# Output projection and down projection with channels on the partitions, in a hybrid encoder layer

## The chip, the cores and the metric

One Trainium2 chip, one core. The metric is the device time of one execution in microseconds. Several executions give a median; one more is recorded by the hardware profiler, and its trace gives the busy times, the waits and the timeline quoted below.

## The reference

One encoder layer over 2048 tokens of 1024 channels in float32: three token mixers on one normalised input, gated and summed to y; then an output projection into the residual stream and an MLP with squared relu. Only the end matters here:

```python
y = (gates[:, :, 0] * (h_m @ w_proj_mlstm)
     + gates[:, :, 1] * (h_na @ w_proj_na)
     + gates[:, :, 2] * (h_mem @ w_proj_mem))
x = x + y @ w_out                                # (2048, 1024)
u = rmsnorm(x, g_ffn) @ w_up                     # (2048, 4096)
return x + jnp.square(jax.nn.relu(u)) @ w_down
```

rmsnorm divides by the root of the mean square over channels, plus 1e-6, and multiplies by the gain g_ffn.

## The kernel before

**Precision.** Every large product is three matmuls (`mm3`, L230): an operand is split into a rounded high part and the rest (ScalarE copies the high part, VectorE subtracts), and high x high, high x low and low x high are summed in PSUM. These are lines L235 to L237. A split of 512 columns is thus one ScalarE and one VectorE instruction.

**Phases.** Phase 1 computes the input projections, the neighbourhood and memory attention; phase 2 the mLSTM; phase 3 the rest, for two pairs of blocks of 512 tokens (blocks 3 and 2, then 1 and 0). A pair goes through four stages:

- `merge` multiplies the three branch outputs with their projections, weights stationary, applies the gates, and leaves yT: channels on partitions, 512 tokens along, high and low. The first block's yT lies in the buffer `hT`, the second's in the buffers that are later b21 (high) and t4 (low).
- `out_proj` (L1342) multiplies by w_out. Now a tile of 128 tokens of yT is stationary and 512 output channels of w_out are moving, so the result has tokens on partitions: 2 halves of the channels x 2 blocks x 4 token tiles = 16 groups of 24 matmuls. Each group adds x (L1364), multiplies by g_ffn along the channels (L1366), stores the new x to scratch `x2`, and sums squares by ScalarE with an accumulator (L1370).
- `operands` (L1379), queued as a job, transposes each result by four matmuls with the identity (L1386), since the MLP wants channels on partitions, and makes from it the operands of a Strassen product in Winograd's form: the token half (block) and channel half give b11, b21, b12, b22 and sums t1 to t4, each split into high and low (`split`, L1390; `less`, L1394; `more`, L1401).
- `mlp_up` (L1423), 16 times per pair: seven products of 12 matmuls, sums on VectorE, squared relu (L1457), results and their sums to scratch. `mlp_down` (L1470): seven products again for each of 4 quarters of the hidden width, 48 matmuls each, summed in `acc` (L1535); here hidden activations are stationary and w_down moving, so tokens are on partitions. In the last quarter, four of the products are the last for their part of the output: x2 is loaded (L1540), one multiply-add scales by the reciprocal mean square of the token, a scalar per partition, and adds x2 (L1542), and the result is stored. The root is absent because relu is squared.

**What sets the order.** TensorE runs in the order of the program. `tick`, called after every second step of a product, runs one entry of a list of jobs; `operands` of a group is entered so that it comes at least `LATER_3 = 4` ticks after it, about one group. The other engines' queues, and SyncE's, which issues all DMAs, are ordered ahead of time by a list scheduler: by readiness and by a priority that follows the program, with a few shifts (eviction `SOON` = 40 earlier, weight splits `LATER` = 60 later, mlp_down's splits `LATER_A` = 60 later). Buffers with waiting users: five for split weights (`WSP`), eight of 128x512 for evictions (`ev`), eight PSUM banks. mlp_down prefetches its operands six steps ahead, in the first pair four and then two steps ahead towards the end, when buffers are given to the next merge (`rings`).

`u` is a buffer in the place of hT that holds mlp_up's sums (`utmp`, `usum`) and two result tiles (`uout`). `gbc` is 128x1024 and holds g_ffn on all partitions in this phase.

Of the kernel before, what the change touches and what calls it, by code (L numbers as in the profile page):

```python
# [13 lines left out]
F32 = mybir.dt.float32  # L14
F32R = mybir.dt.float32r
BF16 = mybir.dt.bfloat16
AF = mybir.ActivationFunctionType
# [5 lines left out]
D = 1024  # L23
# [28 lines left out]
def units(g):  # L52


    def navm(w):
        return [(np.concatenate([w[q:q + 256, 2064:2576], w[q:q + 256, 1536:1552]], axis=1)
                 .reshape(2, 128, 528).transpose(1, 0, 2), 2) for q in range(0, 1024, 256)]

    def ch(w):
        return [(w[:, c:c + 128].reshape(8, 128, 128).transpose(1, 0, 2), 8) for c in range(0, w.shape[1], 128)]  # L60

    def tok(w):
        return [(w[q:q + 256, c:c + 512].reshape(2, 128, 512).transpose(1, 0, 2), 2)
                for c in range(0, w.shape[1], 512) for q in range(0, w.shape[0], 256)]
    win = g["w_in"]
    return dict(w_mem_kv=tok(g["w_mem_kv"]), naqk=tok(win[:, 1552:2064]), qk=ch(win[:, 0:512]),
                v=tok(win[:, 512:1024]),
                gate=ch(win[:, 2576:5648]), o=tok(win[:, 1024:1536]),
                proj=ch(np.concatenate([g["w_proj_mlstm"], g["w_proj_na"], g["w_proj_mem"]])),
                w_out=tok(g["w_out"]), up=ch(g["w_up"]), down=tok(g["w_down"]), navm=navm(win))  # L70

# [12 lines left out]
class Body:  # L84
# [206 lines left out]
    def scratch(self):  # L291
# [19 lines left out]
            hT={b: d(f"s_hT{b}", [128, 2, 8, TB]) for b in SPILL},  # L311
            x2=[d(f"s_x2{b}", [TB, D]) for b in range(NB)],

# [953 lines left out]
    def phase_3(self):  # L1267
# [10 lines left out]
        mix = [[planes("b11"), planes("t2")], [planes("t3"), planes("b22")]]  # L1278
        self.ss = self.p_a.tile([128, 2, 16], F32, name="ss3")
        self.r2 = self.p_a.tile([128, 16], F32, name="r23")  # L1280
# [8 lines left out]
        for i in range(0, NB, 2):  # L1289
# [5 lines left out]
            self.merge(pair, mix, yT)  # L1295
            self.out_proj(pair, yT)

            u = self.p_h.tile([128, 8192], F32, name=f"u{i}", tag="hT", bufs=1)
            self.utmp = [u[:, k * 512:k * 512 + 512] for k in range(4)]
            self.usum = u[:, 2048:4096].rearrange("p (s t) -> p s t", s=4)  # L1300
            self.uout = [u[:, 4096 + k * 2048:6144 + k * 2048].rearrange("p (u i t) -> p u i t", u=2, i=2) for k in range(2)]
            for q in range(FF // 256):
# [38 lines left out]

    def out_proj(self, pair, yT):  # L1342

        nc, a = self.nc, self.a
        for half in range(2):
            w = self.take(4)
            hs = slice(half * 512, half * 512 + 512)
            for j, b in enumerate(pair):  # L1350
                for t in range(4):
                    x = self.ev()
                    r0 = b * TB + t * 128
                    nc.sync.dma_start(x, a["x"][r0:r0 + 128, hs])
                    p = self.ps("mm")
                    ts = slice(t * 128, (t + 1) * 128)
                    for k in range(8):
                        wk = w[k // 2]
                        self.mm3(p, (yT[j][0][:, k, ts], yT[j][1][:, k, ts]), (wk[:, 0, k % 2], wk[:, 1, k % 2]), k == 0, k == 7)
                        if k % 2:  # L1360
# [3 lines left out]
                    nc.vector.tensor_tensor(x, x, p, ALU.add)  # L1364
                    xh = self.ev()
                    nc.vector.tensor_tensor(xh, x, self.gbc[:, hs], ALU.mult)  # L1366
                    self.tc.cur_priority += SOON
                    self.store(self.scr["x2"][b][t * 128:(t + 1) * 128, hs], x)
                    n = 4 * b + t
                    nc.scalar.activation(self.t("ev", [128, 512], EV[3], BF16), x, AF.Square, accum_out=self.ss[:, half, n:n + 1])  # L1370
                    self.jobs += [None] * (LATER_3 - len(self.jobs) - 1)
                    self.jobs.append(lambda xh=xh, half=half, j=j, t=t: self.operands(xh, half, j, t))
        for b in pair:
            r = self.r2[:, 4 * b:4 * b + 4]
            nc.vector.tensor_tensor(r, self.ss[:, 0, 4 * b:4 * b + 4], self.ss[:, 1, 4 * b:4 * b + 4], ALU.add)
            nc.vector.tensor_scalar(r, r, 1.0 / D, EPS, ALU.mult, ALU.add)
            nc.vector.reciprocal(r, r)

    def operands(self, xh, half, j, t):  # L1379


        nc, X = self.nc, self.X
        ts = slice(t * 128, (t + 1) * 128)
        p = self.ps("mm").rearrange("p (a b) -> p a b", b=128)
        for i in range(4):
            nc.tensor.transpose(p[:, i], xh[:, i * 128:(i + 1) * 128], self.ident)  # L1386
        part = lambda x, l: X[x][:, l, :, ts]
        f32 = lambda x, l: part(x, l).bitcast(F32)

        def split(x, src):  # L1390
            nc.scalar.activation(part(x, 0), src, AF.Copy)
            nc.vector.tensor_tensor(part(x, 1), src, f32(x, 0), ALU.subtract)

        def less(src, x):  # L1394

            e = self.ev().rearrange("p (a b) -> p a b", b=128)
            nc.vector.tensor_tensor(e, src, f32(x, 0), ALU.subtract)
            nc.vector.tensor_tensor(e, e, f32(x, 1), ALU.subtract)
            return e

        def more(x, src):  # L1401

            e = self.ev().rearrange("p (a b) -> p a b", b=128)
            nc.vector.tensor_tensor(e, f32(x, 0), src, ALU.subtract)
            nc.vector.tensor_tensor(e, e, f32(x, 1), ALU.add)
            return e
        if half == 0 and j == 0:

            split("t1", p)
        elif half == 0:  # L1410
            split("b11", p)
            split("t1", more("t1", p))
        elif j == 0:
            t2 = less(p, "t1")
            split("b22", p)
            split("t2", t2)
            split("t3", less(t2, "b11"))
        else:
            t4 = less(p, "t2")
            split("b21", p)  # L1420
            split("t4", t4)

# [47 lines left out]
    def mlp_down(self, i, pair, then):  # L1470
# [43 lines left out]
        for q in range(0, FF // 256, 4):  # L1514
            for _, _, s, more, out in products:
                for dq in range(4):
                    if dq % 2 == 0:
# [11 lines left out]
                last = q == FF // 256 - 4 and (out, s, more) in ((0, 1, False), (3, 0, True), (1, 1, True), (2, 0, True))  # L1529
                for t, p in enumerate(sets[s]):  # L1530
                    c = acc[:, out, t]
                    if out not in seen:
                        nc.scalar.activation(c, p, AF.Copy)
                    else:
                        nc.vector.tensor_tensor(c, c, p, ALU.add)  # L1535
                    if last:
                        j, half = out // 2, out % 2
                        hs, r0 = slice(half * 512, half * 512 + 512), t * 128
                        x = self.ev()
                        nc.sync.dma_start(x, self.scr["x2"][pair[j]][r0:r0 + 128, hs])  # L1540
                        n = 4 * pair[j] + t
                        nc.vector.scalar_tensor_tensor(x, c, self.r2[:, n:n + 1], x, ALU.mult, ALU.add)  # L1542
                        r0 += pair[j] * TB
                        self.store(self.a["out"][r0:r0 + 128, hs], x)
                seen.add(out)
# [42 lines left out]
def layout(inp):  # L1588
# [9 lines left out]
        x=g["x"], mem=g["mem"], g_mix=bc(g["g_mix"]), gT_mix=g["g_mix"].reshape(8, 128).T,  # L1598
        xT=g["x"].reshape(16, 128, 8, 128).transpose(0, 3, 2, 1).reshape(16, 128, D), g_ffn=bc(g["g_ffn"]), g_mem=g["g_mem"].reshape(8, 128).T, memT=g["mem"].T,
        w_units=wu, w_navm=wn, b_if=bif,  # L1600
# [22 lines left out]
```

## Time and profile before

| | |
|---|---|
| median of 3 runs | 2894.17 us (2893.63 to 2894.92) |
| profiled execution, its own time | 2894.83 us |
| its span, first to last instruction | 2893.1 us |
| mean granted TensorE clock | 0.998 |
| VectorE (DVE) busy | 2004.3 us |
| ScalarE (ACT) busy | 1187.3 us |
| phase 3, first projection group to last instruction | from 1388.78 us on |

How to read the lines: a group of instructions stands as line, engine, operation, output <- inputs, shapes and count, then busy time in us and mean ns of one, then the idle time ahead of it and what ended it. A timeline row is start, duration, engine, line, operation, tiles, count, and in brackets the idle time before it with its releaser. Tiles carry the program's names without numbers, and some are named by the buffer that they share: ws are split weights, wr raw ones, mm a PSUM bank, X and B the buffers of the Strassen operands. L235 to L237 stand in a helper and are told apart by their tiles.

### The profile page before, as it was taken

Reading aid. Unit: us, or ns where it says so; the run is one execution under the profiler, and the core shown is the slowest. Engines: PE = TensorE matmul, PEld = TensorE weight load, DVE = VectorE, ACT = ScalarE, POOL = GpSimd, SP = SyncE. Lnnn points to the kernel's source line nnn. Section 1 sums busy time; section 2 is a strip of 40 time slices with the busy share of each in tenths; the row PEclk is TensorE's granted clock in tenths of the full one; section 3 lists DMA queues with packets and bytes.
Section 4 is the critical chain, followed back from the end, with each engine's and each line's share of the span. In section 5 each row is a group of like instructions: output and inputs, shape, how many; then the busy total and the mean of one; then the engine's idle time right before and its main releaser. Section 6 shows DMA issues by size and latency. Waiting matters only on the chain.

```text
span 2893.1 us, 41875 instructions
## 1 busy us (share of the span) xinstructions
PE 2861.0 (99%) x15052; PEld 2364.8 (82%) x15052; DVE 2004.3 (69%) x3438; ACT 1187.3 (41%) x2256; POOL 216.4 (7%) x382
## 2 busy tenths in 40 slices
PE   8999999999999999999999999999999999999999
PEld 6878788878877888888888888888888888888887
DVE  6676765567765555647598888666785988885666
ACT  7465654344543443532243334443322433344331
POOL 4121310011000122310000000000000000000000
PEclk9999999999999999999999999999999999999999
DMA  8786778877899888978344446656863444476654
GB/s 281 227 270 203 226 231 259 259 222 231 270 306 299 269 258 283 308 261 272 117 137 158 160 146 238 224 189 228 301 205 113 144 148 160 151 249 202 196 188 160
DMA packets 345153, 632.79 MB, mean 219 GB/s; under 512 B 29456, under 2 KB 151248, under 8 KB 344944
## 3 DMA queue, kind: packets, MB, share of 16 engines
q1 hardware_dynamic: 344944, 630.10, 67.5%
q8 instruction: 119, 1.95, 0.3%
q14 instruction: 90, 0.74, 0.1%
HBM read 453.37 MB, written 176.62 MB: 218 GB/s over the span
## 4 chain that ended last, share of the span: by engine, by line
PE 89%; DVE 3%; issue 3%; DMA 3%; ACT 1%; POOL 0%; SPq 0%; DVEq 0%; POOLq 0%; ACTq 0%
PE mm L235 27%; PE mm L237 27%; PE mm L236 27%; PE tr L1105 1%; PE pn L882 1%; PE mx L1086 1%; PE mx L1119 1%; PE pn L885 1%; PE mx L891 1%; DVE ws L180 1%; DMA nav<-s_vna 1%; PE mx L1258 1%; PE tr L1248 1%; DMA xt<-in_xT_dram 0%; DMA wr<-in_w_units_dram 0%
## 5 line engine op out<-in xcount | busy, mean ns | idle before, releaser
L235 PE MATMUL mm<-X,ws 128*128 128x512 f32 x896 | 349.0, 389 | 0.0
L237 PE MATMUL mm<-X,ws 128*128 128x512 f32 x896 | 348.6, 389 | 0.0
L236 PE MATMUL mm<-X,ws 128*128 128x512 f32 x896 | 348.6, 389 | 0.0
L180 DVE TENSOR_TENSOR ws<-wr,ws 128x1024 fp32r<-128x1024 f32 (+1 forms) x194 | 240.0, 1244 | 127.4 <-ACT ws L179 126.2
L235 PE MATMUL mm<-hT,ws 128*128 128x512 f32 (+1 forms) x712 | 283.0, 397 | 0.7 <-ACT ev L565 0.7
L237 PE MATMUL mm<-hT,ws 128*128 128x512 f32 (+1 forms) x712 | 277.0, 389 | 0.0
L236 PE MATMUL mm<-hT,ws 128*128 128x512 f32 (+1 forms) x712 | 276.7, 389 | 0.0
L235 PE MATMUL mm<-ws,hT 128*128 128x512 f32 (+2 forms) x704 | 258.3, 367 | 3.5 <-ACT zif L529 2.7
L237 PE MATMUL mm<-ws,hT 128*128 128x512 f32 (+2 forms) x704 | 249.6, 355 | 2.2 <-DVE hT L438 2.2
L179 ACT ACTIVATE ws<-wr 128x1024 fp32r<-128x1024 f32 (+1 forms) x194 | 204.1, 1058 | 111.1 <-PE mm L237 76.0
L236 PE MATMUL mm<-ws,hT 128*128 128x512 f32 (+2 forms) x704 | 248.7, 353 | 0.0
L237 PE MATMUL mm<-X 128*128 128x512 f32 x616 | 239.7, 389 | 0.2 <-DVE X L1509 0.2
L236 PE MATMUL mm<-X 128*128 128x512 f32 x616 | 239.6, 389 | 0.0
L235 PE MATMUL mm<-X 128*128 128x512 f32 x616 | 239.6, 389 | 0.0
L205 ACT ACTIVATE ws<-wr 128x512 fp32r<-128x512 f32 x224 | 135.0, 628 | 220.1 <-PE mm L237 139.5
L1508 ACT ACTIVATE X<-X 128x1024 fp32r<-128x1024 f32 x109 | 115.6, 1062 | 202.6 <-DMA X<-s_a 67.2
L237 PEld LDWEIGHTS mm<-X,ws 128*128 128x128 f32 x896 | 168.2, 188 | 35.0
L235 PEld LDWEIGHTS mm<-X,ws 128*128 128x128 f32 x896 | 168.2, 188 | 34.9
L236 PEld LDWEIGHTS mm<-X,ws 128*128 128x128 f32 x896 | 168.2, 188 | 34.8
L1509 DVE TENSOR_TENSOR X<-X 128x1024 fp32r<-128x1024 f32 x109 | 132.6, 1223 | 79.0 <-ACT X L1508 78.5
L1535 DVE TENSOR_TENSOR acc<-acc,mm 128x512 f32<-128x512 f32 x192 | 126.5, 683 | 64.8 <-PE mm L237 64.8
L235 PEld LDWEIGHTS mm<-hT,ws 128*128 128x128 f32 x712 | 134.0, 188 | 28.9 <-issue 4.3
(286 smaller groups left out, 5985.6 us busy)
## 6 DMA issues: line engine op xcount, KB each, us to landing
wr<-in_w_units_dram SPq DMA_DIRECT2D x290, 512.0 KB
s_s<-u SPq DMA_DIRECT2D x32, 1024.0 KB
s_g<-ev SPq DMA_DIRECT2D x96, 256.0 KB
ev<-s_g SPq DMA_DIRECT2D x96, 256.0 KB
s_a<-u SPq DMA_DIRECT2D x96, 256.0 KB
X<-s_s SPq DMA_DIRECT2D x45, 512.0 KB
nab<-in_rpb_dram SPq DMA_DIRECT2D x96, 220.0 KB
xt<-in_w_units_dram SPq DMA_DIRECT2D x32, 512.0 KB
```

The costliest lines, as they stand in the source:

```text
L179: nc.scalar.activation(w[:, 0], raw, AF.Copy)
L180: nc.vector.tensor_tensor(w[:, 1], raw, w[:, 0].bitcast(F32), ALU.subtract)
L205: nc.scalar.activation(hi, src, AF.Copy)
L235: mm(out, lhs[0], rhs[0], start=first, stop=False)
L236: mm(out, lhs[0], rhs[1], start=False, stop=False)
L237: mm(out, lhs[1], rhs[0], start=False, stop=last)
L882: mm(pn[h % 2][:, h // 2], pt[:, h], v1[:, h], start=h < 2, stop=first)
L885: mm(pn[h % 2][:, h // 2], qw[hp, h // 2], C[hp, h // 2], start=False, stop=True)
L891: nc.tensor.matmul(pu[hp, h // 2], kw[:, h], v1[:, h], start=True, stop=True)
L1508: nc.scalar.activation(hi, src, AF.Copy)
L1509: nc.vector.tensor_tensor(lo, src, hi.bitcast(F32), ALU.subtract)
L1535: nc.vector.tensor_tensor(c, c, p, ALU.add)
```

## The change

- w_out is packed in units of 128 output channels, so that it is the stationary operand; yT, 512 tokens, is moving. The result has channels on partitions, 8 channel tiles x 2 blocks = 16 groups of 24 matmuls per pair. x is read from a transposed copy among the inputs (`xC`), and x2 is stored by channels.
- No transpositions. g_ffn becomes a scalar per partition (`gffn`) inside the instructions that make the operands.
- Squares are made by ScalarE into a tile, summed over channel tiles on VectorE in `gbc`, and summed over partitions by one float32 matmul with a matrix of ones per block (`inverse`), which leaves the mean square on all partitions; the reciprocal is of 128x512.
- The last four results (second half, second block) are staged in `uout[1]`; `u` is therefore taken before that stage. Their operand steps, for b21 and then t4, are jobs that run in the first mlp_up, since b21 and t4 still hold yT until the projection ends.
- mlp_down takes w_down stationary and activations moving. A last product loads x2 ahead of it, multiplies `acc` by the inverse and adds it to x2 ahead of the product too; behind it the PSUM result is multiplied by the inverse, added and stored.
- The output leaves as (1024, 2048) and is transposed on the host's side.

```diff
-                w_out=tok(g["w_out"]), ...
+                w_out=ch(g["w_out"]), ...
...
-            x2=[d(f"s_x2{b}", [TB, D]) for b in range(NB)],
+            x2=[d(f"s_x2{b}", [8, 128, TB]) for b in range(NB)],
...
-        nc.sync.dma_start(self.gbc, a["g_ffn"])
+        nc.sync.dma_start(self.gffn, a["gT_ffn"])
...
+    def out_proj(self, pair, yT, i):
+        nc, a = self.nc, self.a
+        stage = None
         for half in range(2):
+            ws = self.take(4)
             for j, b in enumerate(pair):
+                if half and j:
+                    self.up_tiles(i)
+                    stage = self.uout[1].rearrange("p u i t -> p (u i) t")
+                sq = self.gbc[:, j * TB:(j + 1) * TB]
+                for k, w in enumerate(ws):
+                    c = 4 * half + k
                     x = self.ev()
+                    nc.sync.dma_start(x, a["xC"][c, :, b * TB:(b + 1) * TB])
                     p = self.ps("mm")
+                    for n in range(8):
+                        self.mm3(p, (w[:, 0, n], w[:, 1, n]), (yT[j][0][:, n], yT[j][1][:, n]), n == 0, n == 7)
+                        if n % 2:
                             self.tick()
+                    to = x if stage is None else stage[:, k]
...
+                    nc.vector.tensor_tensor(to, x, p, ALU.add)
...
+                    x = to
+                    self.store(self.scr["x2"][b][c], x)
+                    if c == 0:
+                        nc.scalar.activation(sq, x, AF.Square)
+                    else:
+                        e = self.ev()
+                        nc.scalar.activation(e, x, AF.Square)
+                        nc.vector.tensor_tensor(sq, sq, e, ALU.add)
+                    if stage is None:
+                        self.operands(x, half, j, k)
+                if half:
+                    self.jobs += [None] * (LATER_3 - len(self.jobs) - 1) + [lambda sq=sq: self.inverse(sq)]
+        for name in ("b21", "t4"):
+            for k in range(4):
+                self.jobs.append(lambda name=name, k=k, x=stage[:, k]: self.operands(x, 1, 1, k, name))
+
+    def inverse(self, sq):
+        nc = self.nc
+        p = self.ps("mm")
+        nc.tensor.matmul(p, self.ones, sq, start=True, stop=True)
+        nc.vector.tensor_scalar(sq, p, 1.0 / D, EPS, ALU.mult, ALU.add)
+        nc.vector.reciprocal(sq, sq)
+
+    def operands(self, x, half, j, k, late=None):
...
+        g = self.gffn[:, 4 * half + k:4 * half + k + 1]
...
+            split("t1", x, g)
         elif half == 0:
+            split("b11", x, g)
+            split("t1", less(x, "t1", g), -1.0)
         elif j == 0:
+            t2 = less(x, "t1", g)
+            split("b22", x, g)
             split("t2", t2)
             split("t3", less(t2, "b11"))
+        elif late == "b21":
+            split("b21", x, g)
         else:
+            split("t4", less(x, "t2", g))
...
 # mlp_down
             for _, _, s, more, out in products:
+                last = q == FF // 256 - 4 and (out, s, more) in ((0, 1, False), (3, 0, True), (1, 1, True), (2, 0, True))
+                if last:
+                    j, h0 = pair[out // 2], out % 2 * 512
+                    r2, xs = self.gbc[:, out // 2 * TB:(out // 2 + 1) * TB], [self.ev() for _ in range(4)]
+                    for t, x in enumerate(xs):
+                        nc.sync.dma_start(x, self.scr["x2"][j][out % 2 * 4 + t])
+                        c = acc[:, out, t]
+                        nc.vector.tensor_tensor(c, c, r2, ALU.mult)
+                        nc.vector.tensor_tensor(x, x, c, ALU.add)
...
-                        self.mm3(p, (at[:, 0, d, ts], at[:, 1, d, ts]), (at[:, 0, 2 + d], at[:, 1, 2 + d]),
+                        self.mm3(p, (at[:, 0, 2 + d, ts], at[:, 1, 2 + d, ts]), (at[:, 0, d], at[:, 1, d]),
                                  not more and dq == 0, dq == 3, more)
...
                     c = acc[:, out, t]
+                    if last:
+                        nc.vector.tensor_tensor(c, p, r2, ALU.mult)
+                        nc.vector.tensor_tensor(xs[t], xs[t], c, ALU.add)
+                        self.store(self.a["out"][h0 + t * 128:h0 + t * 128 + 128, j * TB:(j + 1) * TB], xs[t])
+                    elif out not in seen:
                         nc.scalar.activation(c, p, AF.Copy)
                     else:
                         nc.vector.tensor_tensor(c, c, p, ALU.add)
```

More of the change, by code (lines that the diff above doesn't have):

```diff
@@ L69, in units @@
                 proj=ch(np.concatenate([g["w_proj_mlstm"], g["w_proj_na"], g["w_proj_mem"]])),
-                w_out=tok(g["w_out"]), up=ch(g["w_up"]), down=tok(g["w_down"]), navm=navm(win))
+                w_out=ch(g["w_out"]), up=ch(g["w_up"]), down=tok(g["w_down"]), navm=navm(win))
 def unit_index():
@@ L1278, in phase_3 @@
         mix = [[planes("b11"), planes("t2")], [planes("t3"), planes("b22")]]
-        self.ss = self.p_a.tile([128, 2, 16], F32, name="ss3")
-        self.r2 = self.p_a.tile([128, 16], F32, name="r23")
+        self.gffn = self.p_a.tile([128, 8], F32, name="gffn")
         order = list(reversed(range(NB)))
@@ L1295, in phase_3 @@
             self.merge(pair, mix, yT)
[L1296 to L1301, printed above, removed]
+            self.out_proj(pair, yT, i)
             for q in range(FF // 256):
@@ L1340, in merge @@
                 nc.vector.scalar_tensor_tensor(lo, acc, 0.5, hi.bitcast(F32), ALU.mult, ALU.subtract)
-    def out_proj(self, pair, yT):
+    def out_proj(self, pair, yT, i):
         nc, a = self.nc, self.a
+        stage = None
         for half in range(2):
-            w = self.take(4)
-            hs = slice(half * 512, half * 512 + 512)
+            ws = self.take(4)
             for j, b in enumerate(pair):
-                for t in range(4):
+                if half and j:
[4 more added lines that the diff above has]
+                    c = 4 * half + k
@@ L1369, in out_proj @@
[L1369 to L1377, printed above, removed]
@@ L1379, in operands @@
-    def operands(self, xh, half, j, t):
-        nc, X = self.nc, self.X
[L1383 to L1405, printed above, removed]
+                    x = to
@@ new lines, in out_proj, with split, less @@
+        for name in ("b21", "t4"):
[8 more added lines that the diff above has]
+    def operands(self, x, half, j, k, late=None):
+        nc, X = self.nc, self.X
+        g = self.gffn[:, 4 * half + k:4 * half + k + 1]
+        part = lambda n, l: X[n][:, l, k]
+        f32 = lambda n, l: part(n, l).bitcast(F32)
+        def split(n, src, scale=None):
+            if scale is None:
+                nc.scalar.activation(part(n, 0), src, AF.Copy)
+                nc.vector.tensor_tensor(part(n, 1), src, f32(n, 0), ALU.subtract)
+            else:
+                nc.scalar.activation(part(n, 0), src, AF.Copy, scale=scale)
+                nc.vector.scalar_tensor_tensor(part(n, 1), src, scale, f32(n, 0), ALU.mult, ALU.subtract)
+        def less(src, n, scale=None):
+            e = self.ev()
+            if scale is None:
+                nc.vector.tensor_tensor(e, src, f32(n, 0), ALU.subtract)
+            else:
+                nc.vector.scalar_tensor_tensor(e, src, scale, f32(n, 0), ALU.mult, ALU.subtract)
+            nc.vector.tensor_tensor(e, e, f32(n, 1), ALU.subtract)
@@ L1423, in mlp_up, with up_tiles @@
+    def up_tiles(self, i):
+        u = self.p_h.tile([128, 8192], F32, name=f"u{i}", tag="hT", bufs=1)
+        self.utmp = [u[:, k * 512:k * 512 + 512] for k in range(4)]
+        self.usum = u[:, 2048:4096].rearrange("p (s t) -> p s t", s=4)
+        self.uout = [u[:, 4096 + k * 2048:6144 + k * 2048].rearrange("p (u i t) -> p u i t", u=2, i=2) for k in range(2)]
     def mlp_up(self, i, q):
@@ L1535, in mlp_down @@
                         nc.vector.tensor_tensor(c, c, p, ALU.add)
[L1536 to L1544, printed above, removed]
                 seen.add(out)
@@ L1598, in layout @@
         x=g["x"], mem=g["mem"], g_mix=bc(g["g_mix"]), gT_mix=g["g_mix"].reshape(8, 128).T,
[L1599 removed]
+        xT=g["x"].reshape(16, 128, 8, 128).transpose(0, 3, 2, 1).reshape(16, 128, D), xC=g["x"].T.reshape(8, 128, S), gT_ffn=g["g_ffn"].reshape(8, 128).T, g_mem=g["g_mem"].reshape(8, 128).T, memT=g["mem"].T,
         w_units=wu, w_navm=wn, b_if=bif,
@@ L1617 @@
         a[k] = nc.dram_tensor(f"in_{k}_dram", v.shape, mybir.dt.from_np(v.dtype), kind="ExternalInput").ap()
-    a["out"] = nc.dram_tensor("out_0_dram", (S, D), F32, kind="ExternalOutput").ap()
+    a["out"] = nc.dram_tensor("out_0_dram", (D, S), F32, kind="ExternalOutput").ap()
     with tile.TileContext(nc) as tc:
```

23 lines of the change are left out of this document (1 added, 22 removed).

## The prediction

> **What bounds the kernel now.** I read the page first: engine shares, slices, granted clock, chain.
>
> ```profile
> PE 2861.0 (99%) x15052; PEld 2364.8 (82%) x15052; DVE 2004.3 (69%) x3438; ACT 1187.3 (41%) x2256; POOL 216.4 (7%) x382
> PE   8999999999999999999999999999999999999999
> PEclk9999999999999999999999999999999999999999
> PE 89%; DVE 3%; issue 3%; DMA 3%; ACT 1%; POOL 0%; SPq 0%; DVEq 0%; POOLq 0%; ACTq 0%
> ```
>
> TensorE is busy 2861.0 of 2893.1 us, at nine tenths of the clock or more in every slice, and it carries 89% of the chain of waits. So an instruction that leaves TensorE's queue shortens the run by the time between issues that it took, provided that no other engine is late there. VectorE, with 69% over the whole span, is the engine to fear; its share must be read stage by stage.
>
> The change touches the last phase only, so I went to the groups of TensorE instructions by line and shape, and to the timeline of one output projection. In the groups, the number after the bar is the union of busy time, the next the mean duration.
>
> ```profile
> L1386 PE MATMUL mm<-ident,ev 128*128 128x128 f32 x128 | 19.3, 273 | 0.2 <-DVE ev L1366 0.2
> L459 PE MATMUL tr<-zna,ones 128*128 128x512 f32 x6 | 3.1, 592 | 0.0
> ```
>
> ```profile
> 1388.78 0.39 PE L235 MATMUL mm<-ws,hT 128*128 128x512 f32 x1
> ...
> 1399.43 0.40 PE L237 MATMUL mm<-ws,hT 128*128 128x512 f32 x1
> 1399.67 0.60 PE L1386 MATMUL mm<-ident,ev 128*128 128x128 f32 x4
> 1400.02 0.48 PE L235 MATMUL mm<-ws,hT 128*128 128x512 f32 x1
> 1400.34 0.40 PE L236 MATMUL mm<-ws,hT 128*128 128x512 f32 x1
> ...
> 1405.61 0.60 PE L1386 MATMUL mm<-ident,ev 128*128 128x128 f32 x4
> ```
>
> The reader is to look at starts, not durations. From the first matmul of the output projection (1388.78) to the 48th (1399.43) are 47 intervals: 10.65 / 47 = 0.2266 us each, though one lasts 0.39. Durations overlap. The same holds for the 273 ns of a transposition.
>
> **The change part by part.** The sum is made against the profiled execution's own 2894.83 us (span 2893.1), which lies 0.66 us above the median of 2894.17; differences go onto the median.
>
> *Transpositions out.* From one set of four (1399.67) to the next (1405.61) are 5.94 us; 24 matmuls alone are 24 x 0.2266 = 5.44. A set costs 0.50 us, and 128 / 4 = 32 sets cost 16.0 us, all on TensorE's own path. Taken: -16.0. [...]
>
> *The last set's wait.* It waits for VectorE's product with g_ffn:
>
> ```profile
> 1489.04 0.66 PE L1386 MATMUL mm<-ident,ev 128*128 128x128 f32 x4 [0.16 <-DVE ev L1366]
> ```
>
> That is 0.16 us, once. It goes: -0.2. What is late next there is costed below.
>
> *Four matmuls with ones in.* The kernel has three of the same form, in phase 1:
>
> ```profile
> 78.38 0.30 PE L237 MATMUL mm<-ws,hT 128*128 128x272 f32 x1
> 78.52 1.02 PE L459 MATMUL tr<-zna,ones 128*128 128x512 f32 x2
> 78.97 0.69 PE L235 MATMUL mm<-ws,hT 128*128 128x272 f32 x1
> 79.50 0.29 PE L236 MATMUL mm<-ws,hT 128*128 128x272 f32 x1
> 79.62 0.29 PE L237 MATMUL mm<-ws,hT 128*128 128x272 f32 x1
> ```
>
> L237 to L236 takes 1.12 us around it; two steps of 0.12 (79.50 to 79.62) would have passed anyway, so one costs 0.88 us. Four: +3.5. Bounds: 0.45 (78.52 to 78.97, the starts alone) and 1.02 (the records, whole), so 1.8 to 4.1 for four; the interval of the same rows is the nearest, so 3.5 stays.
>
> *Same matmuls, other operands.* The projection keeps 16 x 24 matmuls per pair, and mlp_down keeps its products with stationary and moving sides exchanged; the shapes stay 128x128 against 128x512, of which the whole last phase consists, with weights on either side. Nothing is taken. w_out's units by channels free their buffers one by one instead of all in the last group: a help for the weights of the first mlp_up.
>
> *VectorE in the projection.* Out go 32 products with g_ffn; in come 28 sums of squares of the same size and the gain moves into instructions that exist. ScalarE does 32 squares as before. No cost.
>
> *The 8 operand steps moved into the first mlp_up.* Today b21 and t4 are made token tile by token tile, while the projection of the second block runs. Channel by channel they overwrite what the projection still reads as moving operand, so they run after it: 4 splits and 4 times (difference in two, split), 4 + 12 = 16 VectorE and 8 ScalarE instructions per pair, plus the inverse (scale, reciprocal). Who waits: mlp_up's sixth product for b21, its seventh for t4, and the whole matmul queue behind these. Prices and the room that there is:
>
> ```profile
> 1482.80:1502.00 19.20, 19.04 (x88) 15.57 (x87) 18.95 (x35) 10.57 (x19) 0.00 (x0) 1.00 0.63 196
> 1502.00:1521.00 19.00, 19.00 (x85) 15.73 (x84) 17.74 (x29) 6.00 (x10) 0.00 (x0) 1.00 0.54 177
> 1540.00:1559.00 19.00, 19.00 (x86) 15.73 (x85) 15.60 (x25) 6.00 (x10) 0.00 (x0) 1.00 0.45 154
> ```
>
> ```profile
> 1482.30 0.68 DVE L212 TENSOR_TENSOR wr<-wr,wr 128x512 f32<-128x512 f32 x1
> 1482.89 0.68 DVE L206 TENSOR_TENSOR ws<-wr,ws 128x512 fp32r<-128x512 f32 x1
> ```
>
> ```profile
> L1093 DVE RECIPROCAL sm<-sm 128x1 f32<-128x1 f32 x128 | 20.4, 159 | 40.2 <-ACT nsb L1091 39.9
> L1238 DVE RECIPROCAL sm<-sm 128x2 f32<-128x2 f32 x32 | 5.2, 163 | 11.9 <-ACT me L1236 11.7
> L906 DVE RECIPROCAL sm<-sm 128x4 f32<-128x4 f32 x32 | 5.7, 177 | 1.0
> L1366 DVE TENSOR_TENSOR ev<-ev,gbc 128x512 f32<-128x512 f32 x32 | 21.9, 686 | 0.3
> ```
>
> The windows' columns are length, then busy time of PE, PEld, DVE, ACT, POOL. One mlp_up is 84 x 0.2266 = 19.0 us. A settled one keeps VectorE busy 15.60 of 19.00 us; the first keeps it busy 18.95 of 19.20 and hands a rest to the second (17.74), yet TensorE loses only the 0.16 above. VectorE's instructions of 128x512 follow each other by 0.60 us. The reciprocal of 128x512 is new. Its low end is one such instruction, 0.69. The high end is the slope of the three small ones: (177 - 159) / 3 = 6 ns per element, 0.16 + 511 x 0.006 = 3.2 us. I take 3.2, because the slope is of the same operation. [...]
>
> Now deadlines, counted from the projection's end. t4's last plane is wanted nine matmuls into the seventh product, at 6 x 12 x 0.2266 + 2.0 = 18.4 us. By then VectorE must have done the last eviction and sum of squares, 16 operand instructions, four of mlp_up's sums, one weight split (23 x 0.60 = 13.8) and, if it comes first, the inverse (0.6 + 3.2): 17.6 us. It fits by 0.8. The next mlp_up's second product wants s2 at 19.0 + 2.7 = 21.7 us; the fifth sum, two splits, three sums of weights and s2's split are 7 more, 4.2: 21.8 us. No slack at all, and four squared relus in front would add 2.4. So TensorE loses 0 to 4 us at each of the two boundaries; I take 1, nearer to zero because today's first mlp_up, at 99% of VectorE, loses almost nothing: +2.0.
>
> The matmul with ones for the second block stands at mlp_up's fourth tick, 24 x 0.2266 = 5.4 us after the projection; eviction, square and sum before it are three instructions of about 0.65, so it need not wait. The tile u is taken earlier, for the staging; its first write comes after the 24 matmuls of a group that no longer read yT in hT: no cost.
>
> *mlp_down's last products.* Four of the seven products of the last quarter now have, per pair, 16 VectorE instructions instead of 8, eight of them ahead of the product.
>
> ```profile
> 2018.00:2095.40 77.40, 76.04 (x335) 62.31 (x334) 55.26 (x66) 25.37 (x24) 0.00 (x0) 1.00 0.87 299
> 2810.00:2887.00 77.00, 76.89 (x340) 63.33 (x338) 47.93 (x61) 17.94 (x17) 0.00 (x0) 1.00 0.49 164
> L1540 SPq DMA_DIRECT2D ev<-s_x x32: 319/394/665, 1488.2 to 2871.8; - x32
> 2088.42 0.39 PE L235 MATMUL mm<-B 128*128 128x512 f32 x1
> 2090.01 0.50 PE L236 MATMUL mm<-B 128*128 128x512 f32 x1 [1.20 <-DVE B L1509]
> ```
>
> Added are 4 x 8 x 0.60 = 19.2 us per pair. Ahead of the second merge VectorE idles 77.4 - 55.3 = 22.1 us, so it fills to 96%; at the end it idles 29.1, which holds it. TensorE already waits 1.20 us at 2090 for a split that stood behind evictions, with operands prefetched only two ahead there. The bounds are -1.2 (that wait vanishes in the new order) and +6 (a block of eight, 4.8 us, in front of such a split, and the 1.2 again). I take +2.0, nearer to the present wait. The loads of x2 move ahead of the products on SP's queue, past the loads of the next operands; the first is issued at 1488.2 already, half a millisecond early, so the queue is not held up.
>
> *The tail.* After the last matmul today come 4 evictions and 4 multiply-adds:
>
> ```profile
> 2884.62 0.24 PE mm L237
> 2884.89 0.74 DVE acc L1535 x2
> ...
> 2888.69 0.74 DVE ev L1542
> ```
>
> The changed kernel has 4 products and 4 sums in the same 4.8 us: 0.
>
> Sum: -16.0 - 0.2 + 3.5 + 2.0 + 2.0 = -8.7 us. 2894.83 becomes 2886.1, and on the median 2894.17 - 8.7 = **2885.5 us**.
>
> **The rivals.** *VectorE hides all of it:* no wait at the boundaries, the one at 2090 gone. -16.0 - 0.2 + 3.5 - 1.2 = -13.9, 2880.3 us; with nothing gone at 2090 2881.5. For it speaks the first mlp_up of today, which lost 0.16 us at 99% of VectorE; against it the exact zero of slack at s2.
>
> *VectorE takes the gain:* 4 us at each boundary and 6 at the merge: -16.2 + 3.5 + 14 = +1.3, 2895.5; with half of these waits or a little more, 2889 to 2892. For it speaks the 96%.
>
> *Slower, the last products queue in program order:* if VectorE runs all 16 instructions of a last product around it instead of in earlier gaps, that stretch holds 16 x 0.60 + 4 splits of 1.2 = 14.4 us against 48 x 0.2266 = 10.9 of matmuls: 3.5 us lost on each of four products in each pair, 28 us in all, -12.7 + 28 = +15.3, 2909 us. It decides once more than 12.7 + 5.8 = 18.5 us are lost. Against it: splits are wanted only two to six steps later, and the loads of L1540 at 1488.2 show that ready instructions are drawn forward.
>
> *A transposition costs its whole duration* (128 x 273 ns = 34.9 us on the path): -34.9 + 3.3 + 4 = -27.6, 2866.6. [...] The period of 5.94 us speaks against it.
>
> That the transpositions do not go is no rival: the new code issues none there.
>
> **How the numbers follow.** The measurement tells about 0.2%, 5.8 us, from no change, so faster means under 2888.4. The forecast, 2883 to 2888.4: 0.48. All hidden, under 2883: 0.27. The gain taken, 2888.4 to 2900: 0.17. Slower: 0.06. Whole durations: 0.02. Faster 0.48 + 0.27 + 0.02 = 0.77, same 0.17, slower 0.06. The range 2880.0 to 2891.5 leaves out slower, whole durations, a third of the gain taken and the edge under 2880: 0.06 + 0.02 + 0.06 + 0.04.
>
> **What would show it.** In the changed profile the projection's groups stand 5.44 us apart and L1386's rows are gone; four pairs of ones records cost 0.9 us each; VectorE is above 95% in the first mlp_up of each pair and TensorE has waits of about 1 us there, named b21, t4 or a weight tile; the reciprocal of 128x512 lasts about 3 us; one wait of 2 to 4 us lies ahead of the second merge. The prediction is wrong if those waits exceed 7 us together, if the projection's groups are longer than 5.5 us, or if time moves in the first 1300 us, which the change does not touch.

## The result, and the profile after

The changed kernel takes 2916.51 us (median of 5 runs, 2914.10 to 2918.19) against 2893.63 us of the kernel before, measured with it: ratio 1.008, interval 1.0068 to 1.0091. It is 23 us slower; the forecast was 8.7 us faster, with 2891.5 as the upper end of the range.

The profiled execution takes 2916.24 us, its span 2914.5. The page after, engine shares and chain of waits by engine:

```profile
PE 2862.8 (98%) x14932; PEld 2361.3 (81%) x14932; DVE 2055.8 (71%) x3494; ACT 1186.9 (41%) x2224; POOL 214.2 (7%) x382
PE 77%; DVE 9%; issue 8%; DMA 4%; ACT 1%; SPq 1%; POOL 0%; DVEq 0%; POOLq 0%; ACTq 0%
```

TensorE has 120 instructions less and yet 1.8 us more of busy time, and the chain of waits has lost 12 points of TensorE, given to VectorE and to issue. The shares alone don't say where. I cut phase 3 at instructions that both kernels have: the first gating product of a merge, ScalarE's copy of a pair's first mlp_up product, its first copy into `acc`, and the end of the last matmul.

| stage | before, us | after, us | difference |
|---|---|---|---|
| up to the first merge | 1314.9 | 1314.2 | -0.7 |
| merge and projection, first pair | 171.7 | 165.4 | -6.3 |
| mlp_up, first pair | 316.6 | 330.9 | +14.3 |
| mlp_down, first pair | 295.5 | 301.6 | +6.1 |
| merge and projection, second pair | 181.2 | 176.0 | -5.2 |
| mlp_up, second pair | 315.5 | 328.8 | +13.3 |
| mlp_down, second pair | 291.5 | 291.2 | -0.3 |
| tail | 6.2 | 6.3 | +0.1 |

The gain in the projections is there. It is lost twice behind the projection, at the start of mlp_up, and once ahead of the second merge.

The first 48 matmuls of the projection, on the timeline after:

```profile
1387.85 0.39 PE L235 MATMUL mm<-hT,ws 128*128 128x512 f32 x1
...
1398.51 0.39 PE L237 MATMUL mm<-hT,ws 128*128 128x512 f32 x1
```

10.66 us for 47 intervals: the same 0.227 us each with the operands exchanged, and no transpositions between.

Around the projection's end, TensorE's timeline:

```profile
1481.94 0.39 PE L237 MATMUL mm<-X,ws 128*128 128x512 f32 x1
1487.10 2.08 PE L1385 MATMUL mm<-gbc,ones 128*128 128x512 f32 x2 [4.77 <-DVE gbc L1372]
1488.18 1.42 PE L235 MATMUL mm<-X,ws 128*128 128x512 f32 x1
1489.40 0.63 PE L236 MATMUL mm<-X,ws 128*128 128x512 f32 x1
1489.82 0.58 PE L237 MATMUL mm<-X,ws 128*128 128x512 f32 x1
1490.24 0.40 PE L235 MATMUL mm<-X,ws 128*128 128x512 f32 x1
```

The matmul with ones waits 4.77 us for the last sum of squares (L1372), with the whole queue behind it. Then the starts lie 0.42 us apart in place of 0.23. The granted clock goes with it; in the windows, whose columns are as in the prediction, the share of full speed stands behind POOL:

```profile
1487.00:1490.00 3.00, 2.90 (x5) 1.69 (x6) 3.00 (x6) 0.63 (x1) 0.00 (x0) 0.50 0.00 0
1507.00:1511.00 4.00, 4.00 (x11) 3.14 (x12) 3.53 (x6) 0.63 (x1) 0.00 (x0) 0.57 0.84 300
2091.00:2096.00 5.00, 0.47 (x2) 0.03 (x1) 5.00 (x8) 1.06 (x1) 0.00 (x0) 0.84 0.95 326
2096.00:2101.30 5.30, 5.00 (x12) 3.94 (x13) 2.60 (x3) 1.06 (x1) 0.00 (x0) 0.51 1.03 403
```

With each of these clusters of waits the granted clock falls to a half: in windows of 1 us it is 0.50 in every one from 1487 to 1490, from 1508 to 1510 and from 2095 to 2101, and 1.00 again from 1511 to 1513 and from 2102 to 2104. As an estimate from the rows above, that lasts 3.4 us at the seventh product (4.00 us at 0.57 are 3.4 at 0.50 and the rest at 1.00), and ahead of the merge some 6.8 us, counting the window before. The second cluster of the first pair is the seventh product, which needs t4:

```profile
1502.02 0.50 PE L236 MATMUL mm<-B,ws 128*128 128x512 f32 x1 [0.48 <-DVE B L1400]
1503.28 0.50 PE L235 MATMUL mm<-B,ws 128*128 128x512 f32 x1 [0.53 <-ACT B L1399]
1504.49 0.50 PE L236 MATMUL mm<-B,ws 128*128 128x512 f32 x1 [0.71 <-DVE B L1400]
...
1506.89 0.51 PE L236 MATMUL mm<-B,ws 128*128 128x512 f32 x1 [0.65 <-DVE B L1400]
```

Each plane of t4 comes just too late, for its high and again for its low part. Why is everything behind? The last evictions of the projection, VectorE and SyncE's queue, from one timeline window, and the DVE rows of an earlier one:

```profile
1457.24 0.68 DVE L1363 TENSOR_TENSOR ev<-ev,mm 128x512 f32<-128x512 f32 x1
...
1466.57 0.68 DVE L1363 TENSOR_TENSOR u<-ev,mm 128x512 f32<-128x512 f32 x1
...
1470.17 3.35 DVE L1387 RECIPROCAL gbc<-gbc 128x512 f32<-128x512 f32 x1
...
1473.98 0.67 DVE L1363 TENSOR_TENSOR u<-ev,mm 128x512 f32<-128x512 f32 x1
```

```profile
1479.92 0.69 DVE L1363 TENSOR_TENSOR u<-ev,mm 128x512 f32<-128x512 f32 x1 [1.64 <-DMA ev<-in_xC_dram]
1480.64 0.33 SPq L105 DMA_DIRECT2D s_x<-u  x1
1481.02 0.42 SPq L1354 DMA_DIRECT2D ev<-in_xC_dram  x1
1484.55 0.69 DVE L1363 TENSOR_TENSOR u<-ev,mm 128x512 f32<-128x512 f32 x1 [0.62 <-DMA ev<-in_xC_dram]
```

Two pieces of the chain of waits lie between these rows:

```profile
1475.53 4.37 DMA ev<-in_xC_dram
...
1481.02 3.51 DMA ev<-in_xC_dram
```

Evictions follow each other by 9.3, 7.4, 5.9 and 4.6 us, where groups of matmuls end every 5.4. In the first two steps VectorE is never idle: it is behind with the operand steps of the group before, with weight splits, and with the first block's reciprocal. In the last two it waits for x: its load (L1354) stands on SyncE's queue right behind the store of x2 (L105), which waits for the eviction before, and then takes 4.37 and 3.51 us to land. Load, landing, eviction and store form a ring, which starts late by VectorE's backlog and then takes about 5 us a turn, so it catches up little.

The third place, ahead of the second merge:

```profile
2096.30 0.79 PE L237 MATMUL mm<-X 128*128 128x512 f32 x1 [4.83 <-DVE X L1523]
```

A low part of an mlp_down operand is 4.83 us late. ScalarE had its high part done at 2090.69, but VectorE ran sums of the last products first, the last four of them (L1538) for the next product:

```profile
2089.63 1.06 ACT L1522 ACTIVATE X<-X 128x1024 fp32r<-128x1024 f32 x1 [6.08 <-DMA X<-s_t]
```

```profile
2092.61 2.49 DVE L1538 TENSOR_TENSOR ev<-ev,acc 128x512 f32<-128x512 f32 x4
2095.02 1.22 DVE L1523 TENSOR_TENSOR X<-X 128x1024 fp32r<-128x1024 f32 x1
```

### The profile page after: what moved, and what is told of

It reads as the page before. It is cut to its first block, busy times and chain, and to the rows that moved or that the text cites. A ratio compares the mean times of both kernels' runs of the same rounds, so it can differ in the third digit from the quotient of the medians.

```text
span 2914.5 us, 41662 instructions
## 1 busy us (share of the span) xinstructions
PE 2862.8 (98%) x14932; PEld 2361.3 (81%) x14932; DVE 2055.8 (71%) x3494; ACT 1186.9 (41%) x2224; POOL 214.2 (7%) x382
## 4 chain that ended last, share of the span: by engine, by line
PE 77%; DVE 9%; issue 8%; DMA 4%; ACT 1%; SPq 1%; POOL 0%; DVEq 0%; POOLq 0%; ACTq 0%
PE mm L235 24%; PE mm L237 23%; PE mm L236 23%; DMA wr<-in_w_units_dram 1%; PE tr L1105 1%; PE pn L882 1%; DVE ws L180 1%; DMA ev<-in_xC_dram 1%; PE pn L885 1%; PE mx L891 1%; PE mx L1119 1%; PE mx L1086 1%; DVE ev L1412 1%; DVE ev L1411 1%; DMA nak<-s_ks 1%
## 5 line engine op out<-in xcount | busy, mean ns | idle before, releaser
L236 PE MATMUL mm<-X,ws 128*128 128x512 f32 x896 | 351.0, 392 | 0.0
L237 PE MATMUL mm<-X,ws 128*128 128x512 f32 x896 | 350.6, 391 | 0.0
L235 PE MATMUL mm<-hT,ws 128*128 128x512 f32 (+1 forms) x776 | 308.9, 398 | 1.3 <-ACT ev L565 0.7
L237 PE MATMUL mm<-hT,ws 128*128 128x512 f32 (+1 forms) x776 | 302.9, 390 | 0.0
L236 PE MATMUL mm<-hT,ws 128*128 128x512 f32 (+1 forms) x776 | 302.5, 390 | 0.0
L237 PE MATMUL mm<-X 128*128 128x512 f32 x616 | 241.1, 391 | 4.8 <-DVE X L1523 4.8
L236 PE MATMUL mm<-X 128*128 128x512 f32 x616 | 240.7, 391 | 0.0
L235 PE MATMUL mm<-ws,hT 128*128 128x512 f32 (+2 forms) x640 | 233.1, 364 | 2.9 <-ACT zif L529 2.2
L237 PE MATMUL mm<-ws,hT 128*128 128x512 f32 (+2 forms) x640 | 225.1, 352 | 2.0 <-DVE hT L438 2.0
L236 PE MATMUL mm<-ws,hT 128*128 128x512 f32 (+2 forms) x640 | 224.2, 350 | 0.0
L236 PEld LDWEIGHTS mm<-X,ws 128*128 128x128 f32 x896 | 169.6, 189 | 36.3 <-issue 1.0
L237 PEld LDWEIGHTS mm<-X,ws 128*128 128x128 f32 x896 | 169.4, 189 | 35.2
L1523 DVE TENSOR_TENSOR X<-X 128x1024 fp32r<-128x1024 f32 x109 | 132.2, 1223 | 59.7 <-ACT X L1522 58.9
L235 PEld LDWEIGHTS mm<-hT,ws 128*128 128x128 f32 x776 | 146.4, 189 | 32.4 <-issue 4.3
L237 PEld LDWEIGHTS mm<-hT,ws 128*128 128x128 f32 x776 | 146.1, 188 | 31.3
```

The source lines that it names most:

```text
L235: mm(out, lhs[0], rhs[0], start=first, stop=False)
L236: mm(out, lhs[0], rhs[1], start=False, stop=False)
L237: mm(out, lhs[1], rhs[0], start=False, stop=last)
L1523: nc.vector.tensor_tensor(lo, src, hi.bitcast(F32), ALU.subtract)
```

## The experiments

My theory: at the boundary two things add up, the inverse (its matmul waits for late sums, its reciprocal delays t4) and the operand steps moved into mlp_up; ahead of the merge it is VectorE's load. Rivals: one of the two alone; SyncE's queue; the mere order in VectorE's queue; or the gain from the transpositions was never there. Times are medians, beside the kernel before on the same chip. In profiles of the same code the stretch ahead of the first merge takes 1308 to 1318 us, so I compare stages where I can.

**Transpositions alone.** The kernel before, with `operands` reading xh itself:

```diff
-        p = self.ps("mm").rearrange("p (a b) -> p a b", b=128)
-        for i in range(4):
-            nc.tensor.transpose(p[:, i], xh[:, i * 128:(i + 1) * 128], self.ident)
+        p = xh.rearrange("p (a b) -> p a b", b=128)
```

> The kernel before, with the 128 transpositions left out and nothing put in their place: the operand steps read the untransposed result, so the operands hold other numbers in the same amount. Theory A (the gain was sized rightly and lost elsewhere): the groups of the projection stand 5.44 us apart, 16 us less, 2877 to 2879. Theory B (the gain was never there, TensorE waits for the operands or evictions instead): less than 8 us.

2877.20 against 2894.84 us, ratio 0.9941 (0.9926 to 0.9955). In the profiles the two stages with projections take 163.8 and 175.4 us, 7.9 and 5.8 less, 13.7 us together; most of the rest, 5.8 us, lies ahead of the first merge, which the edit does not touch. Theory A: the gain is real and, within the interval, of the size forecast.

**Inverse late.** The changed kernel, with

```diff
-                if half:
-                    self.jobs += [None] * (LATER_3 - len(self.jobs) - 1) + [lambda sq=sq: self.inverse(sq)]
+        self.jobs += [None] * 4
         for name in ("b21", "t4"):
...
+        for j in range(2):
+            self.jobs += [None] * 42 + [lambda j=j: self.inverse(self.gbc[:, j * TB:(j + 1) * TB])]
```

> The changed kernel with the two matmuls with ones of a pair, and so scale and reciprocal, queued some 42 and 85 ticks into the MLP instead of at the projection's end; the operand steps stay where they are. Theory A (the inverse is the cause at the boundary: TensorE stands at the matmul with ones for the late sum of squares, and the 3.3 us reciprocal lies ahead of t4): the stage from the projection's end to mlp_down loses 8 to 13 us per pair, 2891 to 2900 in all. Theory B (the 16 operand instructions are the cause): the wait moves to the sixth and seventh product, at most 5 us in all, 2911 or more.

2909.21 against 2894.84, ratio 1.0057 (1.0039 to 1.0075); the mlp_up stages take 326.0 and 324.7 us, 4.9 and 4.1 less than after the change. Neither end: the wait at the matmul with ones is gone, but larger waits for t4 stand in its place.

```profile
1490.52 0.49 PE L235 MATMUL mm<-B,ws 128*128 128x512 f32 x1 [2.33 <-ACT B L1400]
...
1494.19 0.80 PE L235 MATMUL mm<-B,ws 128*128 128x512 f32 x1 [1.30 <-ACT B L1400]
```

This run also prices one such matmul where nothing waits:

```profile
1556.30 0.40 PE L237 MATMUL mm<-B,ws 128*128 128x512 f32 x1
1556.53 1.02 PE L1386 MATMUL mm<-gbc,ones 128*128 128x512 f32 x2
1556.99 0.80 PE L235 MATMUL mm<-B,ws 128*128 128x512 f32 x1
1557.62 0.40 PE L236 MATMUL mm<-B,ws 128*128 128x512 f32 x1
```

1.32 us from L237 to L236, less two steps of 0.227: 0.87, as forecast.

**No late operands.** The changed kernel without the loop over "b21" and "t4" that queues the operand steps.

> The changed kernel without the eight operand steps that run in the first mlp_up of a pair; b21 and t4 keep what the projection read, so the output is made from other numbers. Theory A (the inverse is the cause): the wait of 4.8 us at the matmul with ones stays, the waits at the seventh product go with some 5 us per pair, 2904 to 2910. Theory B (the operand steps are the cause): 9 us or more per pair, 2898 or less.

2904.11 against 2894.84, ratio 1.0034 (1.0021 to 1.0047); mlp_up 324.9 and 323.3 us, 6.0 and 5.5 less, at the lower end of theory A's range. The seventh product waits no more, the matmul with ones nearly as before:

```profile
1484.96 2.08 PE L1382 MATMUL mm<-gbc,ones 128*128 128x512 f32 x2 [4.23 <-DVE gbc L1372]
```

**Both.** Inverses late, and no late operands.

> The changed kernel with late inverses and without the eight late operand steps, so b21 and t4 keep what the projection read and the output is made from other numbers. If inverse and operand steps are all that the boundary lost: no wait of more than 1 us there, each pair's stage from the first product to mlp_down within 2.5 us of the one before the change, 2893 to 2898 with the merge's loss still in it. If late evictions of the projection cost anything else: 2900 or more.

2889.31 against 2894.99, ratio 0.9982 (0.9972 to 0.9992), below the range that I wrote: in its profile the two stages with projections keep 6.9 and 4.9 us, and the stretch ahead of the first merge, which the edits do not touch, happens to be 2.6 us shorter. mlp_up takes 316.4 and 314.9 us, against 316.6 and 315.5 before the change, with two matmuls with ones in it, and TensorE waits for no engine at the boundary. The two edits together account for the whole loss at the boundary; ahead of the merge TensorE still waits 5.74 us.

**Stores on another queue.** `self.store` of x2 and of the output replaced by `nc.gpsimd.dma_start`.

> The changed kernel with the stores of x2 and of the output issued from GpSimd's queue, so that on SyncE's queue no load of x stands behind a store that waits for an eviction. Theory A (that coupling makes the last evictions of the projection late, and with them the sum of squares): the matmul with ones waits 2 us or less in place of 4.8, and each pair's stage from the projection's end to mlp_down is 4 to 8 us shorter, 2901 to 2909. Theory B (VectorE's queue alone makes them late): the waits stay within 1 us, 2913 or more.

2908.97 against 2894.02, ratio 1.0050 (1.0035 to 1.0065); mlp_up 325.5 and 324.4 us. The matmul with ones that stands at the boundary waits no more, without any change to the inverse (the first block's, inside the projection, waits 0.77 us, in the second pair 1.84):

```profile
1478.38 1.02 PE L1385 MATMUL mm<-gbc,ones 128*128 128x512 f32 x2
```

So what kept the last sum of squares late was the ring of load, eviction and store on SyncE's queue (theory A). What remains is t4, for whose high and low parts TensorE now waits 3.8 us in the first pair (2.9 after the change).

**Early operands.** Inverses late, and the eight operand steps called at the projection's end with a priority 100 earlier:

```diff
-                self.jobs.append(lambda name=name, k=k, x=stage[:, k]: self.operands(x, 1, 1, k, name))
+                self.operands(stage[:, k], 1, 1, k, name)
```

> The changed kernel with the inverses late as in the run before of that kind, and the eight operand steps placed at the projection's end with a priority of 100 earlier, in place of jobs at ticks 5 to 12. Theory A (only their place in VectorE's queue, behind the next weights' splits, makes t4 late): the waits at the seventh product go, the stage to mlp_down comes within 3 us of the one before the change, 2895 to 2901. Theory B (VectorE has too much to do there, in whatever order): the weights of the second mlp_up come late in their place, 2905 or more.

2907.46 against 2894.02, ratio 1.0043 (1.0030 to 1.0057); mlp_up 325.8 and 322.2 us, hardly less than with late inverses alone. t4 is in time, and the next weights are late instead:

```profile
1499.58 0.77 PE L235 MATMUL mm<-B,ws 128*128 128x512 f32 x1 [4.63 <-ACT ws L205]
```

Theory B: with evictions that late, VectorE has more to do by the deadlines than it can, in either of the two orders tried.

**The block ahead of the last products, on GpSimd.** `nc.gpsimd.tensor_tensor` for its 8 instructions.

> The changed kernel with the products and sums ahead of mlp_down's last products on GpSimd instead of VectorE. Theory A (the block on VectorE keeps the operand splits ahead of the second merge waiting): the stretch from mlp_down to the second merge is 4 to 6 us shorter, 2910 to 2912. Theory B (the loads behind x2's loads on SP's queue are late): no change there, 2915 to 2918.

2921.11 against 2894.84, ratio 1.0093 (1.0078 to 1.0108): neither theory, slower. GpSimd needs 1.8 us for each, 14 us for the 8 of a product. VectorE's products behind (L1555) wait 10.7 us for them, and its own sums (L1556) take 0.97 us on average, where they took 0.69 after the change:

```profile
L1537 POOL TENSOR_TENSOR acc<-acc,gbc 128x512 f32<-128x512 f32 x32 | 58.3, 1835 | 1518.0 <-DVE acc L1561 1518.0
L1556 DVE TENSOR_TENSOR ev<-ev,acc 128x512 f32<-128x512 f32 x32 | 30.0, 974 | 0.0
L1555 DVE TENSOR_TENSOR acc<-mm,gbc 128x512 f32<-128x512 f32 x32 | 21.4, 685 | 27.4 <-PE mm L237 16.7 <-POOL ev L1538 5.6 <-POOL acc L1537 5.1
```

**Fewer instructions there.** First pair only: sum, product, sum behind the product, 12 instead of 16.

```diff
-                        nc.vector.tensor_tensor(c, c, r2, ALU.mult)
-                        nc.vector.tensor_tensor(x, x, c, ALU.add)
+                        if not then:
+                            nc.vector.tensor_tensor(c, c, r2, ALU.mult)
+                            nc.vector.tensor_tensor(x, x, c, ALU.add)
...
-                        nc.vector.tensor_tensor(c, p, r2, ALU.mult)
+                        if then:
+                            nc.vector.tensor_tensor(c, c, p, ALU.add)
+                        nc.vector.tensor_tensor(c, c if then else p, r2, ALU.mult)
```

> The changed kernel with the first pair's last products of mlp_down followed by sum, product with the inverse and sum (12 VectorE instructions for each in place of 16, none ahead of the product); the second pair is left as it was. Theory A (VectorE is full ahead of the second merge): that stretch, 6 us longer than before the change, is 3 to 6 us shorter, 2910 to 2914. Theory B (the operands' loads are late on SyncE's queue): within 1 us, 2915 or more.

2910.68 against 2894.02, ratio 1.0056 (1.0042 to 1.0069). mlp_down of the first pair and the merge behind it take 299.6 + 173.4 = 473.0 us; 477.6 after the change. Theory A, 4.6 us. The edit takes out four instructions and also moves the block from ahead of the product to behind it; the next run tries the place alone.

**The early block yields.** The same block left as it was, 200 later in priority.

> The changed kernel with nothing but the block ahead of the first pair's last products put 200 later in priority. Theory A (order): the stretch from mlp_down to the second merge is 3 to 6 us shorter, 2910 to 2914. Theory B (load): the block then is late itself and holds the sums behind the product; within 2 us, or longer.

2917.85 against 2894.99, ratio 1.0076 (1.0062 to 1.0090), the stages 303.3 + 175.8 = 479.1 us: no gain (theory B). The split that TensorE waits for (L1523) now stands behind the eight instructions after a product:

```profile
2089.65 1.28 DVE L1557 TENSOR_TENSOR acc<-mm,gbc 128x512 f32<-128x512 f32 x2
2090.84 1.28 DVE L1558 TENSOR_TENSOR ev<-ev,acc 128x512 f32<-128x512 f32 x2
2092.05 1.28 DVE L1557 TENSOR_TENSOR acc<-mm,gbc 128x512 f32<-128x512 f32 x2
2093.24 1.28 DVE L1558 TENSOR_TENSOR ev<-ev,acc 128x512 f32<-128x512 f32 x2
2094.44 1.22 DVE L1523 TENSOR_TENSOR X<-X 128x1024 fp32r<-128x1024 f32 x1
```

**Three edits together:** stores on GpSimd's queue, late inverses with early operands, 12 instructions.

> The changed kernel with the three edits together: stores on GpSimd's queue, late inverses with early operand steps, and the first pair's last sums behind the product. If each A holds and they add up: 2880 to 2888, the 16 us of the transpositions less some 2 to 10 of remaining waits. If the B of the operand steps holds: 2895 to 2903.

2896.33 against 2894.02, ratio 1.0003 (0.9995 to 1.0012): in B's range, but not for its reason. mlp_up comes to 320.1 and 319.1 us, but ahead of the merge TensorE waits 7.33 us. The chain of waits shows a new ring: the output's store takes 6.07 us from GpSimd's queue, x2's load (L1538) needs its buffer, and an operand's load stands behind that on SyncE's queue.

```profile
2063.33 6.07 DMA out_dram<-ev
2069.39 0.02 SPq L1538
...
2069.86 5.75 DMA B<-s_a
```

**Only x2's stores moved:** the same three edits, with the output's stores back on SyncE's queue.

> The kernel of the three edits together, with the output's stores back on SyncE's queue and only x2's stores on GpSimd's. Theory A (ahead of the second merge, x2's loads wait on SyncE's queue for the slow stores of the output and hold the operand loads behind them): the wait of 7.7 us there shrinks to 2 or 3, 2888 to 2892. Theory B (VectorE's block of 12 alone holds the last split): the wait stays at 5 us or more, 2894 or more.

2886.59 against 2894.99, ratio 0.9969 (0.9956 to 0.9983): theory A, a little below its range. This kernel beats the one before the change too. Its waits ahead of the merge are 0.98, 0.94 and 0.58 us, its mlp_up stages 319.2 and 318.0 us, with one wait left in each, for the second mlp_up's weights:

```profile
2277.73 0.47 PE L235 MATMUL mm<-B,ws 128*128 128x512 f32 x1 [2.71 <-ACT ws L205]
```

**The sums yield too:** product and sum behind the first pair's last products put 200 later.

> The kernel of the run above, with product and sum behind the first pair's last products put 200 later in priority, so that operand splits go ahead of them. Theory A (order in VectorE's queue): the waits ahead of the second merge come to 2 us or less in all, and the time is 2 to 5 us under the run above. Theory B (VectorE's load, whatever the order): no difference beyond 1 us.

2884.00 against 2894.99, ratio 0.9967 (0.9956 to 0.9979). The intervals of the two runs overlap, so the times do not tell them apart. The profiles speak against theory A: the waits ahead of the merge are 2.17 and 0.55 us, 2.7 in all where they were 2.5, and the stages ahead of and with the second merge take 297.8 + 176.3 = 474.1 us, 298.6 + 174.1 = 472.7 without the edit.

## Why the prediction was wrong

**Right.** The transpositions' 16.0 us plus the 0.2 of the last set: 17.6 measured alone, between 13 and 21 by the ratio's interval; the profiles show 13.7 in the two stages with projections. The matmul with ones: 0.88 forecast, 0.87 measured. The reciprocal: 3.2 forecast from the small ones' slope, 3.35 measured. The tail, the exchanged operands and the second pair's mlp_down: no cost, as taken.

**The sign that it named.** More than 7 us of waits were to show the prediction wrong. TensorE waits some 22 us in phase 3 of the changed profile: 8.3 and 7.2 at the boundaries of the two pairs, 6.4 ahead of the second merge.

**Wrong: "so it need not wait".** The step on the matmul with ones counted eviction, square and sum from the projection's end, as if VectorE and the load of x stood ready. They did not: the last eviction began at 1484.55, 7.7 us after the group's matmuls, held by the ring of load and store, which had started late behind the work that the block before had left to VectorE. The profile before had the sign of it, in TensorE's and VectorE's timelines:

```profile
1482.55 0.40 PE L237 MATMUL mm<-ws,B 128*128 128x512 f32 x1
```

```profile
1487.11 0.68 DVE L1364 TENSOR_TENSOR ev<-ev,mm 128x512 f32<-128x512 f32 x1
...
1488.31 0.68 DVE L1366 TENSOR_TENSOR ev<-ev,gbc 128x512 f32<-128x512 f32 x1
```

The projection's matmuls ended near 1482.95, their eviction began 4 us later, and the last transpositions, queued 6 us behind those matmuls, still waited 0.16 us for its result. I read 0.16 as a small loss; it was a chain already late, which the transpositions' place in the queue hid. Moving the stores off SyncE's queue ended the wait of the matmul with ones without touching the inverse.

**Wrong: +1 us at each boundary.** The deadlines (17.6 of 18.4 us, 21.8 of 21.7) assumed a VectorE that starts at zero. With a start several microseconds behind, they had to fail, and an account with no slack should not have been taken at the low end. Measured: mlp_up took 14.3 and 13.3 us more in the two pairs, 0.9 of it for the matmul itself. The upper bound of 4 us left out the wait at the matmul with ones and the clock.

**Missing: the clock.** I priced a wait at its length. In the changed profile 32 intervals of phase 3 are about 0.427 us, 0.2 us too long each: 6.4 us in all. The rows that I had read of the profile before do not show it; a window of its phase 1, behind a wait of 1.80 us, does:

```profile
167.00:171.00 4.00, 3.75 (x12) 3.06 (x13) 2.98 (x8) 2.42 (x9) 3.84 (x3) 0.57 0.89 277
```

In this window the matmuls of 512 columns start 0.428 us apart (167.67 to 169.81, five intervals), and the clock granted from 168 to 170 is 0.50. In the changed profile they start 0.427 us apart behind the wait of 4.83 us ahead of the merge (2096.89 to 2100.73, nine intervals), at 0.50 as well. At the seventh product the clock fell with no wait above 0.71 us. I priced no wait with the slower matmuls behind it, and should have.

**Ahead of the merge:** +2.0 taken, +6 as upper bound. mlp_down and merge together are 0.9 us longer than before although they should have gained some 5 to 7 (6.3 in the run with the transpositions alone left out, 7.9 in its first pair, each less a matmul with ones); so about 6 to 8 us were lost, where 2.0 were taken. That VectorE has too much there is shown by the 4.6 us that four fewer instructions per last product give back, while a later place for the same instructions gave nothing. How the rest divides between its order and the loads' late landing stays open.

**The rivals.** "VectorE takes the gain" named the mechanism but not its size. "Slower, the last products queue in program order" had the right sign in the wrong place: the second pair's mlp_down lost nothing, the first pair's some 6 to 8 us instead of 14, and the larger loss lay at the boundaries.

## What to carry to other kernels

Before work that depends on another engine is put into TensorE's queue, look how far behind that engine's last result already is, and what on the DMA queue its inputs wait for. A transposition that was queued late enough had hidden here that VectorE was late (0.16 us of wait); the matmul with ones, queued earlier, met it (4.77 us). A wait of TensorE cost more than its length here: 0.50 of the clock was granted until 1490, 2.9 us beyond the end of that wait. A sum that is wanted late should be queued late, and a store that waits should not share a queue with loads that must be early; but moving every store made a new wait of 7.33 us here. With x2's stores moved, the inverses late, the operand steps drawn forward and four instructions fewer in the first pair's last products, the same change gives 0.3% in place of losing 0.8%.

## What the runs showed of the hardware

The granted clock fell behind short waits too: at the seventh product of the changed kernel no wait was longer than 0.71 us, TensorE was busy 3.10 of 6.00 us, and the clock then was 0.57 from 1507 to 1511. One single wait of 2.71 us, in the run with only x2's stores moved, left the clock at 1.00 from 2274 to 2280, and the matmuls behind it started 0.23 us apart. The length of a wait alone did not decide: in the run with later sums a wait of 2.17 us, with one of 0.55 us close behind, was followed by starts 0.43 us apart, from 2089.98 to 2091.69. What decides stays open.

```profile
1501.00:1507.00 6.00, 3.10 (x10) 1.19 (x8) 6.00 (x11) 1.53 (x3) 0.00 (x0) 1.00 0.80 276
```

```profile
2274.00:2280.00 6.00, 3.29 (x15) 2.46 (x14) 6.00 (x11) 2.95 (x5) 0.00 (x0) 1.00 0.47 131
```

Sums and products of 128x512 in float32 took 1.76 to 1.84 us on average on GpSimd, in the run with the block there, where VectorE took 0.69 in the changed kernel. VectorE's sums of that size behind the products (L1556) took 0.97 us on average in that run, 0.69 in the changed kernel.
